# Fewer, longer reduction steps for the two-pass transfers of a streaming ReLU row sum

## The chip, the core and the metric

One core of one Trainium2 chip runs the kernel. The metric is device time in microseconds (us). Lower is better. The engines that matter here are VectorE (DVE in the profile), ScalarE (ACT), and SyncE (SP), which issues every DMA transfer.

## What is computed

The input is 32 x 512 rows of 1024 float32 values, 67.1 MB. Negative values are set to zero and each row is summed:

```python
relu_x = np.maximum(x, 0)
return np.sum(relu_x, axis=-1).astype(np.float32)
```

The output has 16384 sums, 65.5 KB.

## The kernel before

The 16384 rows are spread over 128 partitions, 128 rows for each partition. They come in from HBM in the order of the work, in transfers of 16 rows per partition (8.39 MB each). There are seven of them, numbered 0 to 6 here (CHUNKS, line 9; transfer 0 is issued as two DMAs). They go into three buffers in turn (`buf`, NB = 3, line 7). The last 16 rows per partition, the tail, come in smaller pieces of 8, 4 and 2 rows (TAIL, line 12), and then two rows cut into four parts (lines 108 to 115).

SyncE issues all of them on one queue. Transfers 0, 1 and 2 go out at once. Before transfer c (c from 3 on) SyncE waits until VectorE has done all reductions of transfer c - 3, whose buffer it overwrites (line 87; `done`, line 73, counts the reductions). The same wait with c = 7 stands ahead of the tail, which uses the buffer of transfer 4. Behind the tail's issues stand a small store of the first rows' sums (line 117, after a transpose by VectorE at line 169), the store of most sums (line 123) and the last store (line 207).

Transfers 0 to 5 are done in two passes. ScalarE rectifies in place, several rows in one instruction (line 145), and raises a semaphore after each step. VectorE waits until the rows it needs are rectified (line 159) and sums several rows in one `tensor_reduce` (line 160). ACT_STEPS (line 10) and DVE_STEPS (line 11) list how many rows each step of each transfer takes. For transfers 0 to 4 the steps make up all 16 rows. For transfer 5 they make up 12; of the other four rows, ScalarE and VectorE each take two, a row at a time, with one instruction that rectifies and sums (helpers at lines 126 to 132; lines 149 to 154). On VectorE these two rows come ahead of its reductions of transfer 5; on ScalarE they come behind its steps.

Transfer 6 and the tail are done in this one-pass way, row by row, alternately on the two engines (lines 173 to 203). Both engines wait for each transfer's landing first.

Of the kernel before, what the change touches and what calls it, by code (L numbers as in the profile page):

```python
# [6 lines left out]
NB = 3  # L7
REGIONS = [1, 111, 16]
CHUNKS = [[(0, 0, 1), (1, 0, 15)]] + [[(1, 16 * c + 15, 16)] for c in range(6)]
ACT_STEPS = [[16], [7, 9], [7, 9], [7, 9], [4, 5, 7], [3, 4, 5]]  # L10
DVE_STEPS = [[4, 5, 7], [7, 4, 5], [7, 4, 5], [7, 4, 5], [4, 5, 7], [3, 4, 5]]
TAIL = [8, 4, 2]
CUT = 912
HEAD = 256
# [2 lines left out]
def bass_relu_sum_kernel(  # L17
# [53 lines left out]

    NTWO = len(ACT_STEPS)
    done = [sum(map(len, DVE_STEPS[: c + 1])) for c in range(NTWO)]

# [63 lines left out]
    for c in range(NTWO):  # L138
        alone = BIG - sum(ACT_STEPS[c])
        act.wait_ge(s_in[c], 16 * len(CHUNKS[c]))  # L140
        r = 0
        ready = []
        for n in ACT_STEPS[c]:
            t = buf[:, c % NB, r : r + n, :]
# [10 lines left out]
        r = seen = 0  # L155
        for n in DVE_STEPS[c]:
            if ready[r + n - 1] > seen:
# [80 lines left out]
```

## Time and profile before

| what | value |
|---|---|
| median of three runs | 160.8 us (160.78 to 161.15) |
| span of the profiled execution | 159.4 us |
| own time of the profiled execution | not given apart from the span |
| VectorE busy | 120.6 us (76%), 59 instructions |
| ScalarE busy | 101.5 us (64%), 54 instructions |
| DMA queue busy | 98.1%, 67.18 MB |
| VectorE reductions (line 160) | 18, 99.4 us |
| ScalarE rectifying steps (line 145) | 13, 80.4 us |

The span runs from the first instruction to the last; the runs' time holds a little more around it. A timeline line gives the start, the length, the engine, the line of the kernel, the operation, the tiles with their shapes (partitions x elements) and the number of instructions merged; in brackets stands the idle time of the engine before it and what ended it. Where several instructions are merged, the length goes from the first's start to the last's end. "SPq" is SyncE's queue of DMA issues. The chain that ended last is followed back from the last instruction, each time to what released it.

### The profile page before, as it was taken

The numbers are of one execution on the slowest core, as the hardware profiler recorded it, in microseconds if no ns is written. First come the engines' busy times: TensorE is split into PE (matmuls) and PEld (weight loads), VectorE is DVE, ScalarE is ACT, GpSimd is POOL, SyncE is SP. The second block draws the span as 40 slices with busy tenths as digits, with TensorE's granted clock in tenths as the row PEclk, the third lists the DMA queues.
The fourth block names the chain that finished last, engine by engine and source line by source line (L and its number), as shares of the span: only waits on it lengthen the run. The fifth ranks groups of instructions, "written<-read, shape, count | busy, mean of one in ns | idle before, by whom it ended". The sixth has DMA issues, their size and how long they took to land.

```text
span 159.4 us, 150 instructions
## 1 busy us (share of the span) xinstructions
DVE 120.6 (76%) x59; ACT 101.5 (64%) x54; POOL 0.2 (0%) x4
## 2 busy tenths in 40 slices
DVE  0000000009999999999999999999999999898995
ACT  3000059980799708996099941999329980496975
POOL 0000000000000000000000000000000000000000
DMA  9997996996996997989979969969969979798994
GB/s 378 493 401 339 493 526 263 526 526 263 526 493 296 526 444 345 526 378 411 526 312 477 526 263 526 526 263 526 526 263 526 444 345 526 321 469 374 417 400 142
DMA packets 2457, 67.18 MB, mean 421 GB/s; under 512 B 536, under 2 KB 792, under 8 KB 1176
## 3 DMA queue, kind: packets, MB, share of 16 engines
q1 hardware_dynamic: 2456, 67.18, 98.1%
q14 instruction: 1, 0.01, 0.0%
HBM read 67.11 MB, written 0.07 MB: 421 GB/s over the span
## 4 chain that ended last, share of the span: by engine, by line
DVE 55%; DMA 34%; ACT 9%; SPq 2%; issue 0%
DVE res L160 54%; DMA buf<-in_x_dram 34%; ACT buf L145 9%; SPq L101 1%; SPq L112 1%; DVE buf L130 0%; DVE seam L130 0%; SPq L91 0%; DVE turned L169 0%
## 5 line engine op out<-in xcount | busy, mean ns | idle before, releaser
L160 DVE TENSOR_REDUCE res<-buf 128x4 f32<-128x4096 f32 (+3 forms) x18 | 99.4, 5596 | 35.5 <-ACT buf L145 35.5
L145 ACT ACTIVATE buf<-buf 128x7168 f32<-128x7168 f32 (+5 forms) x13 | 80.4, 6233 | 46.1 <-DMA buf<-in_x_dram 46.1
L127 ACT ACTIVATE buf<-buf 128x1024 f32<-128x1024 f32 (+2 forms) x19 | 19.0, 999 | 8.9 <-DMA buf<-in_x_dram 8.9
L130 DVE TENSOR_SCALAR_CACHE_REDUCE buf<-buf 128x1024 f32<-128x1024 f32 (+2 forms) x19 | 20.7, 1143 | 1.7 <-DMA buf<-in_x_dram 1.6
L127 ACT ACTIVATION_READ_ACCUMULATOR buf<-buf 128x1 f32 x19 | 3.6, 188 | 0.0
L145 ACT ACT_TABLE_LOAD x1 | 1.3, 1283 | 1.3 <-PEq L223 1.3
L130 DVE DVE_READ_ACCUMULATOR buf<-buf 128x1 f32 x19 | 1.6, 84 | 0.0
L130 DVE TENSOR_SCALAR_CACHE_REDUCE seam<-seam 128x258 f32<-128x258 f32 x1 | 0.4, 421 | 0.0
L127 ACT ACTIVATE seam<-seam 128x114 f32<-128x114 f32 x1 | 0.3, 300 | 0.1
L169 DVE STREAM_TRANSPOSE turned<-res 128x32 f32<-128x32 f32 x1 | 0.2, 211 | 0.0
L127 ACT ACTIVATION_READ_ACCUMULATOR seam<-seam 128x1 f32 x1 | 0.2, 186 | 0.0
L223 POOL MEMSET const-bfloat16-1.0<- 128x1 bf16 x1 | 0.1, 101 | 0.0
L223 POOL MEMSET const-uint8-127<- 128x1 uint8 x1 | 0.1, 101 | 0.0
L223 POOL MEMSET const-float32-0.0<- 128x1 f32 x1 | 0.1, 98 | 0.2 <-issue 0.2
L223 POOL MEMSET const-float32-1.0<- 128x1 f32 x1 | 0.1, 98 | 0.0
L130 DVE DVE_READ_ACCUMULATOR seam<-seam 128x1 f32 x1 | 0.1, 82 | 0.0
## 6 DMA issues: line engine op xcount, KB each, us to landing
buf<-in_x_dram SPq DMA_DIRECT2D x1, 7680.0 KB, 21.1
buf<-in_x_dram SPq DMA_DIRECT2D x1, 4096.0 KB, 25.3
buf<-in_x_dram SPq DMA_DIRECT2D x1, 2048.0 KB, 29.9
buf<-in_x_dram SPq DMA_DIRECT2D x1, 1024.0 KB, 31.9
buf<-in_x_dram SPq DMA_DIRECT2D x1, 512.0 KB, 3.3
buf<-in_x_dram SPq DMA_DIRECT2D x1, 456.0 KB, 32.5
buf<-in_x_dram SPq DMA_DIRECT2D x1, 256.0 KB, 32.7
seam<-in_x_dram SPq DMA_DIRECT2D x1, 184.0 KB, 32.6
```

The source lines that it names most:

```text
L101: sp.dma_start(out=buf[:, tb, r : r + n, :], in_=xv[-1][:, r : r + n, :]).then_inc(s_in[NBIG + i], 16)
L112: sp.dma_start(out=flat[:, lo:hi], in_=rows[:, lo:hi]).then_inc(s_in[NBIG + len(TAIL) + k], 16)
L127: return act.activation(t, t, AF.Relu, accum_out=acc)
L130: return dve.tensor_scalar(out=t, in0=t, scalar1=0.0, scalar2=None, op0=ALU.max, op1=ALU.add, accum_out=acc)
L145: act.activation(t, t, AF.Relu).then_inc(s_act, 1)
L160: dve.tensor_reduce(out=res[:, c * BIG + r : c * BIG + r + n], in_=buf[:, c % NB, r : r + n, :], axis=X, op=ALU.add,).then_inc(s_dve, 1)
L169: dve.transpose(out=turned[:, :], in_=res[:, 0:32]).then_inc(s_turn, 1)
L223: nc = _bacc.Bacc("TRN2", target_bir_lowering=False, num_devices=1)
```

## The change

```diff
-ACT_STEPS = [[16], [7, 9], [7, 9], [7, 9], [4, 5, 7], [3, 4, 5]]
-DVE_STEPS = [[4, 5, 7], [7, 4, 5], [7, 4, 5], [7, 4, 5], [4, 5, 7], [3, 4, 5]]
+ACT_STEPS = [[16], [7, 9], [7, 9], [7, 9], [7, 9], [5, 7]]
+DVE_STEPS = [[16], [7, 9], [7, 9], [7, 9], [7, 9], [5, 7]]
```

ScalarE's steps change for transfers 4 and 5 only: 7 and 9 rows instead of 4, 5 and 7, and 5 and 7 rows instead of 3, 4 and 5. VectorE's steps become the same as ScalarE's in every transfer: 16 rows at once for transfer 0, 7 and 9 for transfers 1 to 4, 5 and 7 for transfer 5. There are 11 reductions instead of 18, and 11 rectifying steps instead of 13. The semaphore counts that SyncE, VectorE and ScalarE wait for follow from the lists; SyncE is still released by the last reduction of a transfer. Buffers, transfers, the tail and the stores are as before.

## The prediction

> **What bounds the kernel now.** I read the page first: the span, the DMA row and the chain that ended last.
>
> ```profile
> span 159.4 us, 150 instructions
> ...
> DMA  9997996996996997989979969969969979798994
> ...
> DVE res L160 54%; DMA buf<-in_x_dram 34%; ACT buf L145 9%; SPq L101 1%; SPq L112 1%; DVE buf L130 0%; DVE seam L130 0%; SPq L91 0%; DVE turned L169 0%
> ```
>
> Two readings compete. The chain gives 54% of the span to line 160, the reductions that the change merges; the DMA row is nearly full throughout (98.1% by the page's queue row). What decides is when the transfers land, so I then read the timeline of ScalarE and VectorE at the places where an engine stood waiting for a transfer.
>
> ```profile
> 40.97 13.95 ACT L145 ACTIVATE buf<-buf 128x7168 f32<-128x7168 f32 x2 [5.50 <-DMA buf<-in_x_dram]
> 60.31 13.95 ACT L145 ACTIVATE buf<-buf 128x7168 f32<-128x7168 f32 x2 [5.39 <-DMA buf<-in_x_dram]
> 79.67 13.95 ACT L145 ACTIVATE buf<-buf 128x7168 f32<-128x7168 f32 x2 [5.41 <-DMA buf<-in_x_dram]
> 99.02 14.04 ACT L145 ACTIVATE buf<-buf 128x4096 f32<-128x4096 f32 x3 [5.40 <-DMA buf<-in_x_dram]
> 118.36 10.63 ACT L145 ACTIVATE buf<-buf 128x3072 f32<-128x3072 f32 x3 [5.31 <-DMA buf<-in_x_dram]
> 137.72 1.22 DVE L130 TENSOR_SCALAR_CACHE_REDUCE buf<-buf 128x1024 f32<-128x1024 f32 x1 [0.42 <-DMA buf<-in_x_dram]
> 147.43 1.22 DVE L130 TENSOR_SCALAR_CACHE_REDUCE buf<-buf 128x1024 f32<-128x1024 f32 x1 [0.51 <-DMA buf<-in_x_dram]
> 152.32 1.22 DVE L130 TENSOR_SCALAR_CACHE_REDUCE buf<-buf 128x1024 f32<-128x1024 f32 x1 [0.24 <-DMA buf<-in_x_dram]
> ```
>
> The first column is the start, the bracket the idle time before it. Transfers 1 to 6 land at 40.97, 60.31, 79.67, 99.02, 118.36 and 137.72 (I number from 0): 19.34 to 19.36 us apart, whether VectorE sat idle (up to 35.50) or worked. 8.39 MB in 19.35 us is 434 GB/s. The last 16 rows land by 156.99, another 19.27 us. So the stream of transfers has one rate and no hole, and it sets the end. The chain does not contradict this; it only follows releases:
>
> ```profile
> 122.07 0.33 SPq L101
> ...
> 124.39 32.60 DMA buf<-in_x_dram
> ```
>
> VectorE releases the tail transfers at 122.07, but these are queued behind transfer 6, which occupies the engines until 137.72; of the 32.60 us most is queueing. The last of these issues is through at 124.87 + 0.44 = 125.31, so this release could come some 12 us later before the queue ran dry. The other releases show the same: transfer 3 is issued at 52.86, while transfer 2 lands at 60.31, so 7.4 us are spare, the least of all.
>
> **The prices.** For VectorE the distance from one reduction's start to the next counts, not the duration, since they overlap.
>
> ```profile
> 35.50 4.42 DVE L160 TENSOR_REDUCE res<-buf 128x4 f32<-128x4096 f32 x1 [35.50 <-ACT buf L145]
> 39.83 13.00 DVE L160 TENSOR_REDUCE res<-buf 128x5 f32<-128x5120 f32 x2
> 45.23 15.13 DVE L160 TENSOR_REDUCE res<-buf 128x7 f32<-128x7168 f32 x2
> 52.75 11.93 DVE L160 TENSOR_REDUCE res<-buf 128x7 f32<-128x7168 f32 x2
> ```
>
> 4, 5 and 7 rows take 4.33, 5.40 and 7.52 us: 1.067 us a row and 0.06 fixed. A merge so saves 0.06 us. By durations instead (3354 ns for 3 rows, 7605 for 7, by shape) the fixed part is 0.166 us, but 0.1 of it lies beside the next instruction. 9 and 16 rows are not in the trace for VectorE. At 1.067 and 0.06 they take 9.66 and 17.13 us; the bounds are no fixed part (9.60, 17.07) and the 3-row duration scaled up (10.06, 17.89). I take the line, as 7 rows are on it, and keep the ends. ScalarE's prices are shown: 7 rows 6.18 us behind a transfer with the next start 6.08 after, 9 rows 7.87, 5 rows 4.36 from start to start.
>
> [...]
>
> **Part by part.** 18 reductions become 11, and 13 two-pass activations 11.
>
> Transfer 0: one reduction for three, from 35.50 to 52.63, not 52.75. Transfers 1, 2 and 3: 7.52 + 9.66 for 7, 4, 5, saving 0.06 each; the transpose keeps its place. VectorE would be through with transfer 3 at 104.71 - 5 x 0.06 = 104.41. All ScalarE steps are ready there: the closest is the 9 rows of transfer 3, done at 85.75 + 7.87 = 93.62, wanted at 94.75. SP is released after the last reduction as before, 0.1 to 0.3 us earlier, with the queue full: nothing.
>
> Transfer 4 gets a **new wait**. Its first ScalarE step has 7 rows, not 4: 99.02 + 6.18 = 105.20. VectorE, ready at 104.41, starts at 105.22 and idles 0.81. It could go on at 112.74, but the 9 rows are ready at 99.02 + 6.08 + 7.87 = 112.97; it starts at 113.00 and ends at 122.66, before at 121.95. That is 0.71 later. Behind the wait stand VectorE's two rows of transfer 5, its reductions, and SP's release of all tail transfers (122.07 becomes 122.8, with 12 us to spare) and then of the small store of the transposed rows, wanted by nobody until the end.
>
> Transfer 5: two rows of 1.14 us to 124.94; ScalarE's 5 rows are done by 122.83, its 7 by 128.90, so neither is waited for. 5.40 + 7.53 lead to 137.87. Transfer 6 lands at 137.71, so VectorE starts it 0.15 late instead of 0.42 early. ScalarE has 6.65 us idle there.
>
> What hides the 0.15: VectorE's waits in the tail, 0.51 us at 147.43, 0.24 at 152.32, 0.15 at 154.84 (154.61 + 0.08 to 154.84) and 0.40 at 157.01, in all 1.30 us. The first swallows it. From 147.43 on all is as before, and the end, the last landing at 156.99 plus two short VectorE steps and a 1.4 us store, doesn't move. With the upper bound for every 9- and 16-row step, VectorE would leave transfer 3 1.63 us later (0.64 + 3 x 0.33), at 106.3, past the new wait, and reach transfer 6 at about 139.1: 1.4 late against 1.30 spare, so +0.1 us. With the lower bound the ScalarE wait takes all back: 0.
>
> Sum: 0 on a profiled span of 159.4. The page has no own time of the profiled execution besides this; the three runs have a median of 160.8, 1.4 more, and I take what lies around the span as unchanged. Forecast **160.8 us**, with 160.4 to 161.2 for this case alone: the runs themselves went from 160.78 to 161.15, and I allow as much below.
>
> **Rivals.**
> A. *VectorE is the bound, as the chain reads.* Then seven merges give 0.4 to 1.1 us (7 x 0.06 to 7 x 0.16): 159.7 to 160.4. For it: 54% of the chain, VectorE without a pause from 35.50 to 137.30. Against: landings 19.35 apart regardless. Chance 0.07.
> B. *Slower: VectorE's lateness behind the new wait on transfer 4 outlasts the tail's spare time.* It decides from 1.3 us late at transfer 6, of which I count 0.15; the missing 1.15 could come from long reductions that run over 1.5% slower per row, or from a stream that is faster without the profiler, which shrinks the spare time. If none of the spare time were there, the cost would be VectorE's whole lateness against before, 137.87 - 137.22 = 0.65 us, 161.45; with long reductions at the upper bound 139.1 - 137.22 = 1.9, 162.7. Against: long ScalarE steps show no loss (16 rows 13.86 us, 0.866 a row; 7 rows 6.17, 0.88), and 1.3 us is much. Chance 0.13.
> C. *The merge frees nothing,* because fixed cost is wholly overlapped: VectorE then leaves transfer 3 at 104.71, still ahead of the wait at 105.22, and all else is as forecast. It is inside the forecast.
>
> **How the numbers follow.** About 0.3%, 0.5 us, is what a measurement of this kernel can tell from no change. Forecast with C 0.80, A 0.07, B 0.13. B can give less than 0.5 us and A too, but the forecast can also stray over it in the runs, so same 0.78, faster 0.08, slower 0.14. The range goes from A's near end, 160.4, to B's near end, 161.45, rounded to 161.4.
>
> **What would show it.** Landings again at 40.97 + k x 19.35 and a last one near 157.0. VectorE: idle of 0.8 and 0.25 us on ScalarE's line 145 at 105.2 and 113.0; reductions of 9 rows near 9.7 us and of 16 near 17.2; transfer 6 begun at 137.8 to 137.9 without a wait for DMA; the wait before the first tail rows down from 0.51 to about 0.36. The prediction is wrong if the landings change their distance, if the queue runs dry before a release, or if VectorE finds no wait left at 157.01.

## The result and the profile after

The changed kernel takes 161.17 us (median of 9 runs, 161.04 to 161.34), the kernel before 160.79 (9 runs, 160.75 to 161.15). The ratio is 1.0023, interval 1.0015 to 1.0032: 0.38 us slower, little, but clear of noise.

The page of the changed kernel, the rows that answer to those of before:

```profile
span 159.5 us, 141 instructions
...
DMA  9997996996996997999979969969969979798994
...
DMA buf<-in_x_dram 52%; DVE res L160 28%; ACT buf L145 17%; SPq L101 1%; SPq L112 1%; DVE buf L130 0%; DVE seam L130 0%; SPq L91 0%
```

The span is what it was, 159.5 for 159.4, and DMA is as full (98.0% busy for 98.1%). The chain looks quite different (54% of reductions became 28%), and this moved nothing: it is only another path through work that ends together. VectorE's two waits on ScalarE, and the landings, in the timeline (start, length, ..., idle time before and what ended it):

```profile
99.10 13.95 ACT L145 ACTIVATE buf<-buf 128x7168 f32<-128x7168 f32 x2 [5.40 <-DMA buf<-in_x_dram]
105.31 7.62 DVE L160 TENSOR_REDUCE res<-buf 128x7 f32<-128x7168 f32 x1 [0.74 <-ACT buf L145]
113.08 9.75 DVE L160 TENSOR_REDUCE res<-buf 128x9 f32<-128x9216 f32 x1 [0.15 <-ACT buf L145]
...
118.45 10.54 ACT L145 ACTIVATE buf<-buf 128x5120 f32<-128x5120 f32 x2 [5.40 <-DMA buf<-in_x_dram]
...
137.80 1.06 ACT L127 ACTIVATE buf<-buf 128x1024 f32<-128x1024 f32 x1 [6.74 <-DMA buf<-in_x_dram]
137.95 1.21 DVE L130 TENSOR_SCALAR_CACHE_REDUCE buf<-buf 128x1024 f32<-128x1024 f32 x1
...
147.51 1.22 DVE L130 TENSOR_SCALAR_CACHE_REDUCE buf<-buf 128x1024 f32<-128x1024 f32 x1 [0.37 <-DMA buf<-in_x_dram]
```

Landings are 19.35 us apart as before (99.10, 118.45, 137.80), all 0.08 later because the first one was. VectorE idles 0.74 and 0.15 us at transfer 4, starts transfer 6 0.15 us after it has landed, and has 0.37 us of idle time before the first tail rows. Everything inside the span goes as forecast.

So the loss is not in the span. Each run has a time and a span. In the nine runs of the changed kernel the spans are 159.4 to 159.7, and the time less the span is 1.67 us on average. In the runs of an unchanged copy (below) spans are 159.3 to 159.6 and the rest is 1.37. I call this rest "outside" (before the first instruction or after the last); 0.30 of the 0.38 us is there. The mean spans, 159.51 and 159.46, differ by less than those of the kernel before do from one series of runs to another (159.46 to 159.52). One thing in the traces goes with it. The page's queue rows before:

```profile
q1 hardware_dynamic: 2456, 67.18, 98.1%
q14 instruction: 1, 0.01, 0.0%
```

and after:

```profile
q1 hardware_dynamic: 2456, 67.18, 98.0%
```

The kernel before has one packet of 8 KB on the instruction queue inside its span (it starts at 159.21 us and takes 0.49), the changed kernel none. I call such a packet a code packet.

### The profile page after: what moved, and what is told of

It is laid out like the page before. It is cut to its first block, busy times and chain, and to the rows that moved or that the text cites. A ratio compares the mean times of both kernels' runs of the same rounds, so it can differ in the third digit from the quotient of the medians.

```text
span 159.5 us, 141 instructions
## 1 busy us (share of the span) xinstructions
DVE 120.3 (75%) x52; ACT 101.3 (64%) x52; POOL 0.2 (0%) x4
## 4 chain that ended last, share of the span: by engine, by line
DMA 52%; DVE 28%; ACT 17%; SPq 2%; issue 0%
DMA buf<-in_x_dram 52%; DVE res L160 28%; ACT buf L145 17%; SPq L101 1%; SPq L112 1%; DVE buf L130 0%; DVE seam L130 0%; SPq L91 0%
## 5 line engine op out<-in xcount | busy, mean ns | idle before, releaser
L160 DVE TENSOR_REDUCE res<-buf 128x7 f32<-128x7168 f32 (+3 forms) x11 | 99.2, 9064 | 36.5 <-ACT buf L145 36.5
L145 ACT ACTIVATE buf<-buf 128x7168 f32<-128x7168 f32 (+3 forms) x11 | 80.2, 7332 | 46.2 <-DMA buf<-in_x_dram 46.2
```

Of the source, the lines that this page charges most:

```text
L145: act.activation(t, t, AF.Relu).then_inc(s_act, 1)
L160: dve.tensor_reduce(out=res[:, c * BIG + r : c * BIG + r + n], in_=buf[:, c % NB, r : r + n, :], axis=X, op=ALU.add,).then_inc(s_dve, 1)
```

## The experiments

Theory L is rival B of the prediction: VectorE's lateness outlasts the spare time. Theory P: the length of the program on an engine decides, through loading of its code at start or end. I give the instructions of VectorE and ScalarE in a program as a pair (an accumulating instruction counted once): 41/37 before, 34/35 after. They are counted in the program; the profile of before lists 39 and 34 of them, and the others do no row work. All runs below are timed in 5 rounds against the kernel before; "outside" is the mean of time less span over a kernel's runs.

**An unchanged copy (41/37).** No edit.

> The kernel before, unchanged, timed as if it were a change. It gives the spread between two copies of one program and the span of each single run, which the trace of before lacks. Theory L (VectorE starts transfer 6 late, and that lateness costs the 0.38 us) and theory P (the length of the program on each engine costs it, outside the row work: loading of code, start and end) both expect a ratio of 1.000 within 0.0010, and 160.8 us. Theory N (the 0.38 us is only how a build happens to fall, nothing that the steps do) expects a ratio that can differ by 0.002. If runs of 160.8 us show a span of some 159.1 us, the lost time lies inside the span; if they show 159.4, outside it.

160.83 us, ratio 1.0002 (0.9993 to 1.0010); span 159.46, outside 1.37. The code packet is in the span again, at 159.31. So the 0.38 us are not what two copies of one program differ by, and they lie outside the span.

**VectorE merged for transfers 0 to 3 only (36/37).**

```diff
-DVE_STEPS = [[4, 5, 7], [7, 4, 5], [7, 4, 5], [7, 4, 5], [4, 5, 7], [3, 4, 5]]
+DVE_STEPS = [[16], [7, 9], [7, 9], [7, 9], [4, 5, 7], [3, 4, 5]]
```

> Only VectorE's steps of transfers 0 to 3 are merged (16; 7 and 9); transfers 4 and 5 keep the steps of before, so no new wait stands at transfer 4. Five reductions fewer. Theory L: 160.8 us, no change, since VectorE comes to transfer 4 some 0.3 us early and is not late anywhere. Theory P: about five ninths of the loss, 161.0, or all of it, 161.17, if it is VectorE's program alone that counts.

161.39 us, ratio 1.0039 (1.0026 to 1.0051): slower than the whole change, with no new wait, and with VectorE early at transfer 6 (0.73 us of idle time before it, 0.42 in the kernel before). Theory L can't give that. Span 159.50, outside 1.93. What the DMA queues did from 159.5 to 162 us, that is, behind this kernel's span (the row has 40 slices of 0.0625 us; the last row is queue: packets, MB, share):

```profile
GB/s 0 0 0 0 0 0 0 0 0 0 0 0 0 0 0 0 0 0 0 0 0 0 0 0 0 131 0 0 0 0 0 0 0 0 0 0 0 0 0 0
DMA packets 1, 0.01 MB, mean 3 GB/s; under 512 B 0, under 2 KB 0, under 8 KB 0
...
q14 instruction: 1, 0.01, 1.2%
```

The code packet comes at 161.1 us, 1.7 us behind the span's end, and not at 159.2 to 159.4 as before. Neither amount of theory P (161.0, 161.17) was right.

**New steps for transfers 4 and 5 only (39/35).**

```diff
-ACT_STEPS = [[16], [7, 9], [7, 9], [7, 9], [4, 5, 7], [3, 4, 5]]
-DVE_STEPS = [[4, 5, 7], [7, 4, 5], [7, 4, 5], [7, 4, 5], [4, 5, 7], [3, 4, 5]]
+ACT_STEPS = [[16], [7, 9], [7, 9], [7, 9], [7, 9], [5, 7]]
+DVE_STEPS = [[4, 5, 7], [7, 4, 5], [7, 4, 5], [7, 4, 5], [7, 9], [5, 7]]
```

> Only transfers 4 and 5 get the new steps (7 and 9; 5 and 7, on both engines); VectorE's steps of transfers 0 to 3 stay as before. Two reductions and two activations fewer, and the new wait at transfer 4. Theory L: the whole loss, 161.17 us, with VectorE 0.15 late at transfer 6. Theory P: about four ninths of it, 160.95, or none if VectorE's program counts by steps of its length.

161.18 us, ratio 1.0022 (1.0014 to 1.0031), the number of theory L. But the span is 159.46 and outside 1.70, so it is not by L's mechanism. The code packet comes at 160.79, behind the span. The two parts alone lose 0.58 and 0.37, together 0.38: they don't add.

**The changed steps, counts restored (41/37).**

```diff
-ACT_STEPS = [[16], [7, 9], [7, 9], [7, 9], [7, 9], [5, 7]]
+ACT_STEPS = [[5, 5, 6], [7, 9], [7, 9], [7, 9], [7, 9], [5, 7]]
...
+    for i in range(7):
+        dve.memset(pad[:, i : i + 1], 0.0)
```

> The changed kernel with the count of instructions of before: VectorE writes seven single columns of a spare tile while it has nothing else to do, ahead of its first reduction, and ScalarE rectifies transfer 0 in three steps (5, 5, 6), not one, which starts VectorE some 0.2 us later and is taken back at the wait of transfer 4. Theory L: 161.17 us as the changed kernel. Theory P: 160.8 us as before.

(`pad` is a spare tile, here and below.) 160.83 us, ratio 1.0001 (0.9992 to 1.0010); span 159.48, outside 1.35. VectorE waits at transfer 4 and starts transfer 6 0.15 us after it has landed, as in the changed kernel:

```profile
105.38 7.62 DVE L163 TENSOR_REDUCE res<-buf 128x7 f32<-128x7168 f32 x1 [0.62 <-ACT buf L148]
113.15 9.75 DVE L163 TENSOR_REDUCE res<-buf 128x9 f32<-128x9216 f32 x1 [0.15 <-ACT buf L148]
...
137.88 1.06 ACT L127 ACTIVATE buf<-buf 128x1024 f32<-128x1024 f32 x1 [6.74 <-DMA buf<-in_x_dram]
138.03 1.21 DVE L130 TENSOR_SCALAR_CACHE_REDUCE buf<-buf 128x1024 f32<-128x1024 f32 x1
```

And the loss is gone. Theory L has fallen; this run carries most of the verdict. The page has the packet again:

```profile
span 159.5 us, 150 instructions
...
q14 instruction: 1, 0.01, 0.0%
```

**Counts restored on one engine alone.** VectorE by seven writes in front (41/35), ScalarE by steps of 5, 5 and 6 for transfer 0 (34/37), VectorE by seven writes at the end of its program (41/35):

```diff
 # pad_vector_front; pad_vector_end has the same loop ahead of sp.wait_ge(s_last, 2)
+    for i in range(7):
+        dve.memset(pad[:, i : i + 1], 0.0)
 # pad_scalar
-ACT_STEPS = [[16], [7, 9], [7, 9], [7, 9], [7, 9], [5, 7]]
+ACT_STEPS = [[5, 5, 6], [7, 9], [7, 9], [7, 9], [7, 9], [5, 7]]
```

> The changed kernel with VectorE's count of instructions alone brought back to that of before: seven writes of single columns of a spare tile ahead of its first reduction. ScalarE keeps two fewer. Theory P in the form that VectorE's program is what counts (its next block of code is fetched too late to be hidden, behind the last store): 160.8 us, and a packet of the instruction queue inside the span, as before. If it is ScalarE's program: 161.2 and no such packet. Theory L, already weak: 161.2.

> The changed kernel with ScalarE's count alone brought back: transfer 0 rectified in steps of 5, 5 and 6 rows. VectorE keeps its seven fewer. If VectorE's program counts: 161.2 to 161.4 us, and no packet of the instruction queue inside the span; if ScalarE's: 160.8 with the packet.

> The changed kernel with seven writes of single columns of a spare tile at the end of VectorE's program, behind its last row sum, where they run beside the last store (1.4 us). If the place of the program's end in the code counts: 160.8 us as with the writes in front. If the number of instructions VectorE has got through by a given time counts (a fetch that starts when it reaches a certain place), it lies between: the writes take some 7 x 0.1 us, so up to 161.2. Theory L: 161.2.

161.23, 161.36 and 161.20 us; ratios 1.0022 (1.0013 to 1.0031), 1.0025 (1.0016 to 1.0035), 1.0019 (1.0010 to 1.0028); spans 159.50 to 159.51; outside 1.71, 1.83 and 1.70. None comes back. With 41 on VectorE the packet is back in the span, at 159.34 and 159.38, so that packet belongs to VectorE's program. Yet this alone doesn't save the 0.3 us, against what I expected: ScalarE's two missing instructions cost as much by themselves. With 34 VectorE instructions and ScalarE's 37 the packet comes at 161.14. Where in the program the seven stand doesn't matter.

**Eight VectorE instructions more (49/37), and two more (43/37), on the kernel before.**

```diff
+    for i in range(8):   # vector_two_more: range(2)
+        dve.memset(pad[:, i : i + 1], 0.0)
```

> The kernel before with eight more VectorE instructions, writes of single columns of a spare tile ahead of its first reduction. If a longer program only moves the fetch of its next block of code to an earlier time, hidden in any case: 160.8 us or up to 0.1 less, with the packet of the instruction queue earlier in the span than 159.2. If each instruction costs something at start or end: 0.05 to 0.4 more.

> The kernel before with two VectorE instructions more, writes of single columns of a spare tile ahead of its first reduction. With eight more, the packet of the instruction queue came at 143 us and the span was 0.6 longer, while outside stayed at 1.36. Theory E: the packet still at the end (160.8) or moved into the last microseconds of the tail, with a span up to 0.6 longer (161.4), outside 1.36 in both. Theory G: outside 1.5 or more.

161.41 and 161.44 us, ratios 1.0033 (1.0020 to 1.0045) and 1.0038 (1.0025 to 1.0050): slower, but by another way. Outside is 1.36 in both, and the spans are 160.06 and 160.08. The packet comes at 143.17 and 151.58, inside the tail. Landings that VectorE waited for, with two more:

```profile
137.76 1.22 DVE L130 TENSOR_SCALAR_CACHE_REDUCE buf<-buf 128x1024 f32<-128x1024 f32 x1 [0.44 <-DMA buf<-in_x_dram]
147.48 1.22 DVE L130 TENSOR_SCALAR_CACHE_REDUCE buf<-buf 128x1024 f32<-128x1024 f32 x1 [0.51 <-DMA buf<-in_x_dram]
153.10 1.22 DVE L130 TENSOR_SCALAR_CACHE_REDUCE buf<-buf 128x1024 f32<-128x1024 f32 x1 [0.98 <-DMA buf<-in_x_dram]
157.67 0.42 DVE L130 TENSOR_SCALAR_CACHE_REDUCE buf<-buf 128x256 f32<-128x256 f32 x1 [0.33 <-DMA buf<-in_x_dram]
```

Up to 147.48 it is the kernel before (there 137.72 and 147.43). The next landing is at 153.10, not 152.32: the packet at 151.58 falls between them, and the wait grew from 0.24 to 0.98. With eight more it is the landing at 148.15 (before: 147.43) that is late, the packet being at 143.17. In both the landing behind the packet comes some 0.7 us late, and the end 0.6 with it. My "hidden in any case" was wrong: here, inside a stream without a hole, neither packet was hidden.

**One ScalarE instruction less (41/36); two VectorE less (39/37); three ScalarE more (41/40),** each on the kernel before.

```diff
 # scalar_one_less: ScalarE's steps of transfer 5
-[3, 4, 5]
+[7, 5]
 # vector_two_less: VectorE's steps of transfer 0
-[4, 5, 7]
+[16]
 # scalar_three_more: ScalarE's steps of transfer 0
-[16]
+[4, 4, 4, 4]
```

> The kernel before with one ScalarE instruction fewer: transfer 5 rectified in steps of 7 and 5 rows, not 3, 4 and 5; VectorE's first reduction there waits some 0.3 us, less than the 0.42 it had to spare. Theory E (what lies outside the span depends on where the end of each engine's code falls, so on its count of instructions, in a step): outside 1.36 us as before, or 1.70 as with two fewer, nothing between; 160.8 or 161.2. Theory G (a cost per missing or added instruction): outside about 1.53, 161.0. The span stays at 159.45.

> The kernel before with VectorE's reduction of transfer 0 in one instruction of 16 rows: two VectorE instructions fewer, ScalarE as before, no new wait. Theory E: outside the span 1.36 or a step of about 0.3 to 0.6 above it, with the late packet of the instruction queue behind the span's end, as in the kernels with 36 and 39 VectorE instructions: 161.2 to 161.4. Theory G: two sevenths of VectorE's share, under 0.2: 160.9 to 161.0.

> The kernel before with ScalarE rectifying transfer 0 in four steps of 4 rows: three ScalarE instructions more, and VectorE starts some 0.3 us later, inside its 0.42 spare. Theory E: outside 1.36 or less, if ScalarE's end part was still partly in the way; a packet of the instruction queue may move into the span, and cost the stream 0.3 to 0.6 us if it falls into the tail. Theory G, in the form that any count other than that of before costs: 161.0 or more, outside the span.

160.97, 161.03 and 160.92 us; ratios 1.0009 (1.0000 to 1.0018), 1.0013 (1.0005 to 1.0022) and 1.0006 (0.9997 to 1.0015, unclear). Spans 159.45 to 159.46; outside 1.52, 1.57 and 1.47. Theory E's clean steps do not show: 37, 36 and 35 on ScalarE give 1.36, 1.52 and 1.70. (The means of 39/37 and 41/40 hide a spread, 1.32 to 1.73 and 1.33 to 1.63; with 41/37 it is 1.33 to 1.41.) Nor does a price for each instruction (theory G): VectorE's two cost 0.2 alone and nothing beside ScalarE's two (1.70 with 39/35 as with 41/35). With 39/37 the packet comes at 160.93; with 41/40 there are two, at 159.31 and at 160.76, the second one new with the longer ScalarE program. It lies behind the span, here from 159.5 to 162 us:

```profile
GB/s 0 0 0 0 0 0 0 0 0 0 0 0 0 0 0 0 0 0 0 0 131 0 0 0 0 0 0 0 0 0 0 0 0 0 0 0 0 0 0 0
...
q14 instruction: 1, 0.01, 0.8%
```

Yet this profile is of a run of 160.84 us, with 1.35 outside: a packet behind the span is not by itself a loss.

**Is there a better count?** One and two ScalarE instructions more (41/38, 41/39), the changed steps with 41/38, and the changed steps with 43/35:

```diff
 # scalar_one_more and scalar_two_more, on the kernel before: transfer 0 on ScalarE
-[16]
+[8, 8]       # scalar_two_more: [5, 5, 6]
 # after_41_38, on the changed kernel: seven writes as above, and transfer 0 on ScalarE
-[16]
+[4, 4, 4, 4]
 # after_43_35, on the changed kernel
+    for i in range(9):
+        dve.memset(pad[:, i : i + 1], 0.0)
```

> The kernel before with ScalarE rectifying transfer 0 in two steps of 8 rows: one ScalarE instruction more. Theory S (each ScalarE instruction less costs 0.17 us around the span, and more gain as much until the next block of code is needed at the end): 1.2 us around a span of 159.45, 160.65. Theory F (37 is on the floor, which something else sets): 1.36, 160.83.

> The kernel before with ScalarE rectifying transfer 0 in steps of 5, 5 and 6 rows: two ScalarE instructions more. Theory S: 1.05 around the span and 160.5, or, if the next block is needed already, 1.5 and 160.95 with a second late packet near 160.8. Theory F: 1.36, 160.83.

> The changed steps with seven writes of single columns of a spare tile on VectorE ahead of its first reduction (41 instructions as before) and transfer 0 rectified in four steps of 4 rows (38 on ScalarE, one more than before). Theory S: 160.65 as the kernel before with one more. Theory F: 160.83. Late start of VectorE at transfer 6 inside the spare time in both.

> The changed kernel with nine such writes on VectorE: 43 instructions there, 35 on ScalarE. If the two engines' parts are independent: VectorE's packet of code inside the tail near 152 us, the span 0.6 longer (160.1), and 1.70 around it from ScalarE: 161.8. If ScalarE's part counts only together with VectorE's late packet: 1.36 around the span, 161.4.

161.00, 160.89, 161.14 and 161.76 us; ratios 1.0016 (1.0007 to 1.0025), 1.0006 (0.9997 to 1.0014), 1.0019 (1.0009 to 1.0028) and 1.0058 (1.0046 to 1.0071). None beats the kernel before; theory S has fallen. With 41/39 too a second packet lies behind the span, at 160.71. With 43/35 the two costs add, as independent ones should: span 160.08 (packet at 151.55) and outside 1.71.

With 41/38 the runs of one program fall into two groups. In the kernel before with one more, six runs have 1.39 to 1.45 outside and five have 1.80 to 1.87, with spans of 159.4 to 159.6 in both. Its profile is of a run of 161.20 us, and behind its span stands a second packet, at 161.1:

```profile
GB/s 0 0 0 0 0 0 0 0 0 0 0 0 0 0 0 0 0 0 0 0 0 0 0 0 0 131 0 0 0 0 0 0 0 0 0 0 0 0 0 0
DMA packets 1, 0.01 MB, mean 3 GB/s; under 512 B 0, under 2 KB 0, under 8 KB 0
...
q14 instruction: 1, 0.01, 0.9%
```

The changed steps with the same counts were profiled in a run of 160.81 us, from the low group, and behind that span (from 159.5 us on) no packet starts:

```profile
DMA packets 0, 0.00 MB, mean 0 GB/s; under 512 B 0, under 2 KB 0, under 8 KB 0
```

Same counts on both engines; one trace with the packet behind the span and 1.8 us outside, one without and 1.4.

## Why the prediction was right and wrong

**What bounds the kernel: right.** Landings stayed 19.35 us apart, and rival A (VectorE is the bound) is out: seven reductions fewer gave no time back, with the counts restored neither (160.83 us, span 159.48).

**The prices: right.** A 9-row reduction takes 9.67 us from start to start (113.08 to 122.75; I had 9.66). By shape the changed kernel's profile has (count, then busy us and mean ns):

```profile
L160 DVE TENSOR_REDUCE res<-buf 128x9 f32<-128x9216 f32 x4 | 39.0, 9745 | 0.2 <-ACT buf L145 0.2
L160 DVE TENSOR_REDUCE res<-buf 128x16 f32<-128x16384 f32 x1 | 17.2, 17221 | 35.6 <-ACT buf L145 35.6
```

so long reductions run on the line of the short ones, and the upper bounds were far off. The 0.16 us a merge behind rival A's 159.7 us is shown by no run as a gain. From start to start the 9 rows took 9.67 us where 4 and 5 rows had taken 9.73, and the 16 rows 17.13 (35.57 to 52.70) where 4, 5 and 7 had taken 17.25: 0.06 us a merge.

**The new wait and the lateness: right,** 0.74 and 0.15 us for 0.81 and 0.25, transfer 6 begun 0.15 late as forecast, 0.37 for 0.36 at the tail, 0.39 for 0.40 at the last wait. The restored counts show that it costs nothing: 160.83 with the same wait.

**The step that failed:** "I take what lies around the span as unchanged." The forecast of 0 was right for the span (159.46 in the copy, 159.51 in the changed kernel, on average) and wrong for the 1.37 us beside it, which became 1.67. I had added that part as a constant without a reason, and looked for slower cases among the engines alone. Rival B had the sign but not the cause. My range held the time because I had widened it for B; that is luck, as the case it came from was not among my cases. I had also taken 0.5 us as the least that a measurement of this kernel can tell; the interval here is 0.14 us to either side.

**Shown: the counts do it.** The loss lies outside the span. All steps are the same with 34/37 and 41/37 on the changed steps, and seven idle writes on VectorE bring outside from 1.83 to 1.35. ScalarE's count changed only together with its steps, but the two that it lost at transfers 4 and 5 are made good by two more at transfer 0 (1.71 with 41/35, 1.35 with 41/37). The new wait costs nothing. A code packet moves with VectorE's count (49, 43, 41, 39 and 36 instructions: 143.2, 151.6, 159.2, 160.9 and 161.1 us).

**Shown: five runs end with a code packet's landing.** The traces have the start and the length of each packet, and in every trace GpSimd's first write starts 0.23 us behind the span's start. For the seven profiled runs with a packet behind the span:

| VectorE/ScalarE | packet starts, us | has landed | run's time + 0.23 | outside in this run |
|---|---|---|---|---|
| 36/37 | 161.12 | 161.60 | 161.60 | 1.95 |
| 34/37 | 161.14 | 161.52 | 161.52 | 1.82 |
| 39/37 | 160.93 | 161.38 | 161.39 | 1.69 |
| 41/38 | 161.09 | 161.43 | 161.43 | 1.75 |
| 41/39 | 160.71 | 161.09 | 161.09 | 1.44 |
| 41/40 | 160.76 | 161.06 | 161.07 | 1.35 |
| 39/35 | 160.79 | 161.15 | 161.32 | 1.69 |

In the first five the two agree to 0.01 us, though the packets take from 0.34 to 0.47 us: counted from that write, the time runs until the packet is in. With 41/40 they agree too, but there the packet is in no later than a run without one ends (1.36 outside), so nothing is lost. In the seventh something else, 0.17 us later, ends the run, and that kernel has 35 on ScalarE.

**Argued:** that in the changed kernel (34/35) the lost time is of this kind too, a code packet that lands late. Its trace shows no such packet up to 162 us. **Open:** what ends the runs with 35 on ScalarE. They have 1.67 to 1.71 outside, and none of their five traces has a second packet. By the 0.23 us one that ended the changed kernel's run would have landed at 161.40, and other traces hold landings up to 161.60, so it isn't simply past the end of the record. Nor is an engine's wait visible: the last semaphore event in these traces comes 1.45 to 1.48 us behind the span's end, as in the copy (1.47). It is later with 41/36 (1.61) and with 36/37 (1.89), so there something did wait. Open too: why 36 on ScalarE costs half of what 35 does, why 34/35 loses less than 34/37, and why a packet of some 0.33 us makes the landing behind it 0.7 late.

The code packets are of 8 KB (131 GB/s in one slice of 0.0625 us), and they go with lost time in two places: 0.6 us in a full stream's tail (spans of 160.06 and 160.08 us for 159.46), and about 0.4 behind the span between the two groups of runs of the kernel before with 41/38 (1.80 to 1.87 outside for 1.39 to 1.45).

## What to carry to other kernels

In this kernel, which streams without a hole, merging instructions off the path gave nothing, and the count of instructions was itself a parameter: two or eight more on VectorE moved a code packet into the stream (0.6 us), and a few fewer on either engine made the part behind the span longer by 0.2 to 0.6 us. Compare time less span as well as the span, look for the instruction queue's row in the page, and bring the counts back with idle instructions before a difference of some tenths of a microsecond is put down to the steps.

## What I had not expected

That two VectorE instructions on idle time, taking nothing from any engine, make a kernel 0.6 us longer (span 160.08 for 159.46), and seven idle writes with two extra ScalarE steps make one 0.34 us shorter (161.17 to 160.83).
